# One more pair by Strassen's scheme, and sums that follow their banks, in a hybrid decoder layer

## The chip, the core and the metric

The kernel runs on one core of a Trainium2 chip. The metric is the device time of one launch in microseconds. Five engines work side by side, each through its own instructions in order: TensorE (PE in the profile; PEld is its load of the stationary operand), VectorE (DVE), ScalarE (ACT), GpSimd (POOL) and SyncE (SP, whose queue issues the DMAs). TensorE writes into eight banks of the accumulator memory (PSUM).

## What is computed

One layer of a decoder for 256 tokens of width 2048, all in f32:

```python
h = rmsnorm(x, norm_mix_g)
u = h @ w_in                       # 2048 x 12288, columns in fields of 1024 or 2048
ya = b_g * causal_dwconv3(c_g * xa, conv_w) * silu(za)
o  = hgrn2_chunked(silu(q), kk, iv, log_f)          # gated recurrence, 8 heads
yb = rmsnorm_per_head(o) * hg_norm_g * silu(og)
m  = sigmoid(ga) * (ya @ w_a_out) + sigmoid(gb) * (yb @ w_b_out)
x  = x + m @ w_o
gate = sigmoid(rmsnorm(x, ple_norm_g) @ w_ple_gate)
x  = x + gate * (p @ w_ple_proj)
return rmsnorm(x, final_norm_g)
```

The matrix products carry nearly all the work. `w_ple_gate` is called the gate in the title of the change and PG in the kernel; `ga` and `gb` are the two merge gates.

## The kernel before

**Products in three passes.** Both operands of a product are split into a high part (rounded to the format that TensorE takes, `F32R`) and a low part (the rest), and a product is the sum of high x high, high x low and low x high. ScalarE makes the high part of the weights (`whi`, L151), VectorE the low one (`wlo`, L152). The 256 tokens are two halves of 128 (t = 0, 1); a bank holds 128 tokens x 512 columns.

**Order of the work.** The columns of all weights are cut into groups of 512; the list `groups` (L169) has them in the order PP (w_ple_proj, whose results are kept in DRAM), the fields of w_in, then for each merge gate column j: ga, gb, A (w_a_out), B (w_b_out), then four groups O (w_o) and four groups PG (w_ple_gate). A group has 8 steps (A and B: 4); a step multiplies a chunk of 256 rows, two tiles of 128, so 2 tiles x 2 token halves x 3 passes = 12 matmuls of 512 columns. The weights come in units of 1 MB, two steps each, into three buffers (`raw`, L106). The split parts sit in a ring of four buffers, five around the pairs of gates (`more`, L206), and ten in PG, where a pool `late` of six joins the four.

**Looking ahead.** Ahead of a step's products, the loop at L1154 asks for all splits up to `ahead(pos)` steps further (L1093): three, four around the pairs, and in PG growing to eight, because the last PG group is multiplied token half by token half and needs all its eight steps split. After the products `ask_ahead` (L1104) asks for the loads of the next units, and `advance` (L1085) moves each open epilogue, a generator, on to its next `yield`. The framework's planner then sets the final order on each engine: it goes by what is ready in its own reckoning, and by program order among that.

**A pair.** For j = 1, 2, 3 the groups ga and gb are one pair GG of 24 steps (`PAIR`, L42). Four of its eight units are joint (`"S"`): one chunk of 256 rows by 1024 columns, that is two row tiles by two column groups, multiplied for both token halves by Strassen's scheme (in Winograd's form) with seven block products for eight. For it the weights are combined (`combine_weights`, L159: three VectorE instructions L163, L166, L167), and so is the left operand (`forms`, L720). A joint unit has four parts with 6, 3, 6 and 6 matmuls. The other four units are plain, each for one of the two column groups. All eight banks are used: four for the results (t, group) and four for the products 1, 5, 6, 7 that several results share. They are asked for at the pair's first step (L1194). `ep_pair` (L754) adds them up; it starts after the last joint unit's fourth part (L1199), and its first adds free the bank that group A needs right after the pair.

**O and PG.** `ep_o` (L816) adds a group of O to x, transposes it by way of DRAM (`turned`) and puts it into `x1T`, PG's left operand, scaled by the norm's gain (`put`, L249). `ep_pg` (L857) takes the sigmoid of a PG group, multiplies it with the kept projection (`load_projection`, L1055, two buffers), adds to x and sums squares; GpSimd multiplies by the final gain (L875). The last group is multiplied in the loop behind the main one (L1257), one bank at a time.

Of the kernel before, what the change touches and what calls it, by code (L numbers as in the profile page):

```python
# [9 lines left out]
F32 = mybir.dt.float32  # L10
F32R = mybir.dt.float32r
# [4 lines left out]
P = 128  # L16
# [25 lines left out]
PAIR = ("S", 0), (0, 2), ("S", 1), (1, 2), ("S", 4), (0, 6), ("S", 5), (1, 6)  # L42
PAIRED = [c for u, c in PAIR if u == "S"]

# [3 lines left out]
PAD_CONST, PAD_SMALL = 8, 64  # L48
# [3 lines left out]
def hybrid_kernel(ctx, tc, xT, x, pT, prm, gfin, masks, w_in, w_a, w_b, w_o, w_pg, w_pp, out):  # L52
# [77 lines left out]
    def split(pos, c0=0, c1=2 * CW):  # L130
# [9 lines left out]
        if more(pos) and pos % (4 + MORE) < MORE:  # L140
            pool, n = pools["tmp2"], MORE
# [29 lines left out]
    for n, (kind, j) in enumerate(IN_ORDER):  # L171
        if j == 0 or kind not in ("ga", "gb"):
            groups.append((kind, j, w_in, n, "hT"))
        elif kind == "ga":
            groups.append(("GG", j, w_in, n, "hT"))
# [14 lines left out]
    for gi, (kind, j, w, g, op) in enumerate(groups):  # L190
        if kind != "GG":
# [3 lines left out]
        for n, (u, c) in enumerate(PAIR):  # L195
# [7 lines left out]
    first_pair = min(pos for pos, s in enumerate(joint) if s)  # L203
    last_pair = max(pos for pos, s in enumerate(joint) if s)

    def more(pos):  # L206

        return first_pair - 12 <= pos <= last_pair + 8
# [511 lines left out]
    def forms():  # L720


        for n in range(0, len(PAIRED), 2):
            raw, f = t4(), t4()
            r = raw.rearrange("p (u k t) -> p u k t", u=2, k=2)
            for u in range(2):
                c = PAIRED[n + u]
                nc.sync.dma_start(out=r[:, u], in_=xT[:, 2 * c : 2 * c + 2, :])
            for u in range(2):
                yield  # L730
                for k in range(2):
                    h = r[:, u, k, :]
                    nc.scalar.activation(
                        out=h, in_=h, func=AF.Identity, scale=gain(PRM_GMIX, 2 * PAIRED[n + u] + k)
                    )
            yield
            a11, a12, a21, a22 = (r[:, :, k, t * P : (t + 1) * P] for t in range(2) for k in range(2))
            s1, s2, s3, s4 = (f[:, i * 2 * P : (i + 1) * 2 * P].rearrange("p (u t) -> p u t", u=2) for i in range(4))
            nc.vector.scalar_tensor_tensor(out=s1, in0=a21, scalar=-1.0, in1=a22, op0=ALU.mult, op1=ALU.subtract)
            nc.vector.scalar_tensor_tensor(out=s2, in0=s1, scalar=-1.0, in1=a11, op0=ALU.mult, op1=ALU.subtract)  # L740
            yield
            nc.vector.tensor_tensor(out=s3, in0=a11, in1=a21, op=ALU.subtract)
            nc.vector.tensor_tensor(out=s4, in0=a12, in1=s2, op=ALU.subtract)
            yield
            hi, lo = (pools["tmp2"].tile([P, 1024], F32R, tag="S" + x, bufs=2, name=nm("S" + x)) for x in "hl")
            nc.scalar.activation(out=hi, in_=f, func=AF.Copy)
            nc.vector.tensor_tensor(out=lo, in0=f, in1=hi.bitcast(F32), op=ALU.subtract)
            for u in range(2):
                for i in range(4):
                    s = slice((2 * i + u) * P, (2 * i + u + 1) * P)  # L750
                    state["S", PAIRED[n + u], i] = hi[:, s], lo[:, s]
            yield

    def ep_pair(j, e, m):  # L754

        ga, gb = t4("ga", 1), t4("gb", 1)
        state["ga", j], state["gb", j] = ga, gb
        a, b = slice(0, CW), slice(CW, 2 * CW)

        def add(out, x, y):  # L760
            nc.vector.tensor_tensor(out=out, in0=x, in1=y, op=ALU.add)

        nc.scalar.activation(out=gb[:, a], in_=m[1], func=AF.Copy)
        add(ga[:, a], gb[:, a], e[0, 0])
        add(gb[:, a], gb[:, a], m[6])
        yield
        add(gb[:, b], gb[:, a], m[7])
        add(ga[:, b], gb[:, b], e[1, 0])
        yield
        pair = gb.rearrange("p (t c) -> p t c", t=2)  # L770
        add(pair, pair, m[5].rearrange("p (o c) -> p o c", o=1).to_broadcast([P, 2, CW]))
        for t in range(NT):
            s = slice(t * CW, (t + 1) * CW)
            nc.scalar.activation(
                out=ga[:, s], in_=ga[:, s], func=AF.Sigmoid, scale=state["rstd1"][:, t : t + 1]
            )
        yield
        for t in range(NT):
            s = slice(t * CW, (t + 1) * CW)
            add(gb[:, s], gb[:, s], e[t, 1])  # L780
        yield
        for t in range(NT):
            s = slice(t * CW, (t + 1) * CW)
            nc.scalar.activation(
                out=gb[:, s], in_=gb[:, s], func=AF.Sigmoid, scale=state["rstd1"][:, t : t + 1]
            )
# [29 lines left out]
    def ep_o(j, psum):  # L816
        xs = state["x"]
        x1 = t4()
        for t in range(NT):
            d = xs[:, t, j * CW : (j + 1) * CW]  # L820
            nc.vector.tensor_tensor(out=d, in0=d, in1=psum[t], op=ALU.add)
# [12 lines left out]
        x1 = yield from turn  # L834
        for c in range(4):
# [21 lines left out]
    def ep_pg(j, psum):  # L857
        xs, pw, gt = state["x"], state["pw", j], t4()
# [493 lines left out]
```

## Time and profile before

| what | value |
|---|---|
| median of 3 runs | 817.11 us (816.95 to 817.17) |
| the profiled execution's own time | 816.79 us |
| its span, first to last instruction | 815.0 us |
| mean granted TensorE clock | 0.996 |
| PE, DVE, ACT, POOL busy | 804.8, 603.9, 455.8, 91.1 us |
| three gate pairs start at | 443.55, 506.26, 569.29 us, 40.80 us each |
| PG starts at, its last group at | 719.04, 784.32 us |
| last matmul ends at | 806.9 us |

Times within the profile count from the span's start. A line such as `L152 DVE TENSOR_TENSOR wlo<-raw,whi ... x302 | 379.8, 1273 | 168.2 <-ACT whi L151` is a group of instructions: kernel line, engine, operation, what it writes and reads, how many; then busy time in us and the mean of one in ns; then the engine's idle time ahead of them, with what ended it. In a table by stage each row is a stretch of the span: its length, each engine's busy time and instructions, the granted clock, the DMA share and GB/s. The chain of waits is followed back from the last instruction.

### The profile page before, as it was taken

The page shows a single profiled execution, that of the slowest core. Times are in us where ns is not written, and L with a number is a line of the kernel's source. Part 1 is how long each engine was busy: PE and PEld are TensorE (multiplying, and loading weights), DVE is VectorE, ACT ScalarE, POOL GpSimd, SP SyncE. Part 2 cuts the span into 40 slices and gives each one's busy share as a digit, 9 for nine tenths or more (in the row PEclk, how much of TensorE's full clock was granted, in tenths as well). Part 3 has the DMA queues.
Part 4 walks back from the last instruction along what each step waited for, and adds up shares of the span by engine and source line. Part 5 has one row for each costly group of instructions (what it writes and reads, how often), then busy time and mean ns, then how long its engine had stood idle before and what let it go on. Part 6 is the DMA issues. An engine that isn't in the chain of part 4 may idle for free.

```text
span 815.0 us, 10926 instructions
## 1 busy us (share of the span) xinstructions
PE 804.8 (99%) x4199; PEld 668.8 (82%) x4200; DVE 603.9 (74%) x711; ACT 455.8 (56%) x596; POOL 91.1 (11%) x75
## 2 busy tenths in 40 slices
PE   9999999999999999999999999999999999999996
PEld 7888888888888888888888888888888888888885
DVE  6746697967766498967768998998996656679734
ACT  7666465555565465465664565554564455567522
POOL 1000045400000055200001001000100000001210
PEclk9999999999999999999999999999999999999998
DMA  9969655647767555748764774774765788887702
GB/s 341 375 267 335 231 176 205 232 158 240 255 236 249 201 178 191 225 153 262 265 232 155 236 278 142 226 272 144 252 256 170 260 296 298 285 285 280 296 1 104
DMA packets 45556, 188.32 MB, mean 231 GB/s; under 512 B 5184, under 2 KB 14656, under 8 KB 29888
## 3 DMA queue, kind: packets, MB, share of 16 engines
q1 hardware_dynamic: 45360, 187.36, 66.1%
q8 instruction: 33, 0.54, 0.3%
q10 hardware_dynamic: 144, 0.26, 0.1%
q14 instruction: 19, 0.16, 0.1%
HBM read 173.97 MB, written 13.63 MB: 230 GB/s over the span
## 4 chain that ended last, share of the span: by engine, by line
PE 93%; DVE 3%; issue 1%; DMA 1%; ACT 1%; ACTq 0%; POOLq 0%; POOL 0%
PE g L1102 80%; PE g L1122 7%; PE s L1122 3%; DVE wlo L152 2%; ACT whi L151 1%; PE s L1102 1%; PE s L448 1%; DMA raw<-in_w_a 1%; DMA raw<-in_w_pp 1%; DVE raw L163 0%; DVE t L166 0%; PE s L581 0%; PE s L604 0%; PE s L605 0%; PE s L603 0%
## 5 line engine op out<-in xcount | busy, mean ns | idle before, releaser
L152 DVE TENSOR_TENSOR wlo<-raw,whi 128x1024 fp32r<-128x1024 f32 (+1 forms) x307 | 382.5, 1262 | 168.4 <-ACT whi L151 165.3
L151 ACT ACTIVATE whi<-raw 128x1024 fp32r<-128x1024 f32 (+1 forms) x307 | 317.1, 1049 | 254.1 <-PE g L1102 205.7
L1102 PE MATMUL g<-wlo,xh 128*128 128x512 f32 (+1 forms) x720 | 276.7, 384 | 0.0
L1102 PE MATMUL g<-whi,xl 128*128 128x512 f32 (+1 forms) x720 | 276.7, 384 | 0.0
L1102 PE MATMUL g<-whi,xh 128*128 128x512 f32 (+1 forms) x720 | 276.3, 385 | 0.0
L1102 PEld LDWEIGHTS g<-whi,xl 128*128 128x128 f32 x720 | 135.3, 188 | 27.0
L1102 PEld LDWEIGHTS g<-wlo,xh 128*128 128x128 f32 x720 | 135.3, 188 | 26.8
L1102 PEld LDWEIGHTS g<-whi,xh 128*128 128x128 f32 x720 | 135.3, 188 | 26.6
L1102 PE MATMUL g<-whi,mh 128*128 128x512 f32 x128 | 49.8, 389 | 0.0
L1102 PE MATMUL g<-wlo,mh 128*128 128x512 f32 x128 | 49.8, 389 | 0.0
L1102 PE MATMUL g<-whi,ml 128*128 128x512 f32 x128 | 49.6, 389 | 0.0
L1122 PE MATMUL g<-whi,xh 128*128 128x512 f32 x120 | 46.7, 389 | 0.0
L1122 PE MATMUL g<-wlo,xh 128*128 128x512 f32 x120 | 46.7, 389 | 0.0
L1122 PE MATMUL g<-whi,xl 128*128 128x512 f32 x120 | 46.7, 389 | 0.0
L151 ACT ACTIVATE whi<-t 128x512 fp32r<-128x512 f32 x12 | 7.6, 634 | 49.5 <-DVE t L166 49.5
L804 POOL TENSOR_TENSOR t<-ga,gb 128x512 f32<-128x512 f32 x6 | 10.6, 1786 | 193.6 <-issue 118.7
L1102 PE MATMUL g<-whi,yaTh 128*128 128x512 f32 (+1 forms) x74 | 28.0, 389 | 1.1 <-ACT whi L151 0.9
L1102 PEld LDWEIGHTS g<-whi,mh 128*128 128x128 f32 x128 | 24.0, 188 | 5.0
L1102 PEld LDWEIGHTS g<-whi,ml 128*128 128x128 f32 x128 | 24.0, 188 | 5.0
L1102 PEld LDWEIGHTS g<-wlo,mh 128*128 128x128 f32 x128 | 24.0, 188 | 4.9
L502 POOL TENSOR_TENSOR t<-b 128x512 f32<-128x512 f32 x10 | 20.3, 2034 | 68.5 <-DMA t<-turn 41.0
L1102 PE MATMUL g<-wlo,yaTh 128*128 128x512 f32 (+1 forms) x74 | 28.0, 384 | 0.0
(202 smaller groups left out, 860.6 us busy)
## 6 DMA issues: line engine op xcount, KB each, us to landing
raw<-in_w_in SPq DMA_DIRECT2D x73, 1024.0 KB, 4.8
raw<-in_w_in SPq DMA_DIRECT2D x34, 512.0 KB, 6.1
raw<-in_w_o SPq DMA_DIRECT2D x16, 1024.0 KB, 5.7
raw<-in_w_pg SPq DMA_DIRECT2D x16, 1024.0 KB, 5.3
turn<-t SPq DMA_DIRECT2D x72, 128.0 KB, 2.6
t<-turn SPq DMA_DIRECT2D x18, 512.0 KB, 5.2
raw<-in_w_a SPq DMA_DIRECT2D x8, 1024.0 KB, 5.2
raw<-in_w_b SPq DMA_DIRECT2D x8, 1024.0 KB, 6.4
```

Of the source, the lines that this page charges most:

```text
L151: a = nc.scalar.activation(out=hi[:, s], in_=src[:, s], func=AF.Copy)
L152: v = nc.vector.tensor_tensor(out=lo[:, s], in0=src[:, s], in1=hi[:, s].bitcast(F32), op=ALU.subtract)
L448: nc.tensor.matmul(heads(bk)[r, h, c if at is None else slice(at, at + 32)], key(h)[:, r], query(h)[:, c], start=True, stop=True, tile_pos ...
L502: nc.gpsimd.tensor_tensor(out=er, in0=br, in1=ref, op=ALU.subtract)
L804: (nc.vector if j == 3 else nc.gpsimd).tensor_tensor(out=spread(m, t), in0=blocks(ga[:, s]), in1=blocks(gb[:, s]), op=ALU.add)
L1102: nc.tensor.matmul(psum, a, b, start=first and n == 0, stop=last and n == 2)
L1122: nc.tensor.matmul(banks[name], x, y[:, s], start=k == total[name] and i == 0, stop=k == 1 and i == 2)
```

## The change

PG's groups 1 and 2 become a pair GP, with its own order of units, `LATE`: plain (group 1, chunks 4 and 5), S0, plain (1, chunks 6 and 7), S1, plain (2, chunks 4 and 5), S2, S3, plain (2, chunks 6 and 7). The joint chunks 0 to 3 lie in the columns of x that O's groups 0 and 1 make, so `ep_o` builds the combined forms of `x1T` there, by the shared `forms`, and writes `x1T` itself as one copy and one subtraction for four chunks. The sums are one generator `sums` for both kinds of pair: it is opened ahead of the first joint unit and goes on as soon as the banks it reads are complete (`left` counts their products down). A bank is asked for at its first product. For GP, `gated` (the old body of `ep_pg`) takes the summed columns instead of banks; projections 1 and 2 are loaded in S0 and S1, projection 3 after the first of the two sums. The look-ahead in PG grows by one each three steps instead of four, and so reaches eight at the 20th of its steps (before: the 25th); the extra buffer around the gates is asked for a little earlier. A pad of 64 words in the small pool goes.

```diff
-PAIR = ("S", 0), (0, 2), ("S", 1), (1, 2), ("S", 4), (0, 6), ("S", 5), (1, 6)
+GATES = ("S", 0), (0, 2), ("S", 1), (1, 2), ("S", 4), (0, 6), ("S", 5), (1, 6)
+LATE = (0, 4), ("S", 0), (0, 6), ("S", 1), (1, 4), ("S", 2), ("S", 3), (1, 6)
-PAD_CONST, PAD_SMALL = 8, 64
+PAD_CONST, PAD_SMALL = 8, 0
...
-        t2 = half[unit_of[pos]] = pools["tmp2"].tile([P, CW], F32, tag="t2", bufs=2, name=nm("t2"))
+        t2 = half[unit_of[pos]] = pools["tmp2" if pos in gates else "tmp3"].tile([P, CW], F32, tag="t2", bufs=2 if pos in gates else 1, name=nm("t2"))
...
-    groups += [("PG", j, w_pg, j, "x1T") for j in range(4)]
+    groups += [("PG", 0, w_pg, 0, "x1T"), ("GP", 1, w_pg, 1, "x1T", LATE), ("PG", 3, w_pg, 3, "x1T")]
...
+    def sums(e, left, tiles_of, then):
+        def until(*names):
+            while any(left[n] for n in names):
+                yield
+        yield from until(1, 6, (0, 0))
+        ga, gb = tiles_of()
+        nc.scalar.activation(out=gb[:, A], in_=e[1], func=AF.Copy)
+        add(ga[:, A], gb[:, A], e[0, 0])
+        add(gb[:, A], gb[:, A], e[6])
+        yield
+        yield from until(7, (1, 0))
+        add(gb[:, B], gb[:, A], e[7])
+        add(ga[:, B], gb[:, B], e[1, 0])
+        yield
+        yield from until(5)
+        both = gb.rearrange("p (t c) -> p t c", t=2)
+        add(both, both, e[5].rearrange("p (o c) -> p o c", o=1).to_broadcast([P, 2, CW]))
+        then(0, ga)
+        yield
+        yield from until((0, 1), (1, 1))
+        add(gb[:, A], gb[:, A], e[0, 1])
+        add(gb[:, B], gb[:, B], e[1, 1])
+        yield
+        then(1, gb)
...
     def ep_o(j, psum):
...
+        if j < 2:
+            for c in range(4):
+                h = x1[:, c * T : (c + 1) * T]
+                nc.scalar.activation(out=h, in_=h, func=AF.Identity, scale=gain(PRM_GPLE, j * 4 + c))
+            hi, lo = (x[:, j * 4 : j * 4 + 4, :].rearrange("p k t -> p (k t)") for x in state["x1T"])
+            nc.scalar.activation(out=hi, in_=x1, func=AF.Copy)
+            nc.vector.tensor_tensor(out=lo, in0=x1, in1=hi.bitcast(F32), op=ALU.subtract)
+            yield
+            r = x1.rearrange("p (u k t) -> p u k t", u=2, k=2)
+            yield from forms("x1T", pools["tmp3"], f"So{j}", r, (2 * j, 2 * j + 1))
+            return
...
+    def ep_gates_late(j, e, left):
+        def then(q, g):
+            gate = gated(j + q, g, [g[:, A], g[:, B]])
+            next(gate)
+            active.append(gate)
+            if q == 0:
+                load_projection(3)
+        yield from sums(e, left, lambda: (t4(), t4()), then)
...
-        return LEAD + min(max(pos - (last_group - 20), 0) // 4, 5) + MORE * (first_pair - 8 <= pos <= last_pair + 8 - MORE)
+        return LEAD + min(max(pos - late - 4, 0) // 3, 5) + MORE * (more(pos + LEAD) is not None and more(pos + LEAD + MORE) == more(pos + LEAD))
...
         def add(name, xh, xl, s):
+            if name not in banks:
+                banks[name] = bank("g" if type(name) is tuple else "s")
...
             if c == (0, 0):
-                left = dict(total)
-                banks = {n: bank("g" if type(n) is tuple else "s") for n in total}
-            pair_products(c)
+                total = products_of(program)
+                left, banks = dict(total), {}
+            if c == (min(n for n, (u, _) in enumerate(program) if u == "S"), 0):
+                active.append({"GG": ep_pair, "GP": ep_gates_late}[kind](j, banks, left))
+            pair_products(c, program, opname)
             ask_ahead()
             if not joint[pos] or c[1] % 2:
                 advance()
-            if c == (max(n for n, (u, _) in enumerate(PAIR) if u == "S"), 3):
-                m = {n: banks[n] for n in (1, 5, 6, 7)}
-                active.append(ep_pair(j, banks, m))
-                step(active[-1])
+            if kind == "GP" and c in ((1, 1), (3, 1)):
+                load_projection(1 + c[0] // 2)
             continue
```

More of the change, by code (lines that the diff above doesn't have):

```diff
@@ L202, in hybrid_kernel @@
     LEAD, MORE = 3, 1
-    first_pair = min(pos for pos, s in enumerate(joint) if s)
-    last_pair = max(pos for pos, s in enumerate(joint) if s)
+    of_kind = lambda *kinds: [pos for pos, (gi, c) in enumerate(steps) if groups[gi][0] in kinds]
+    gates, late = of_kind("GG"), of_kind("PG")[0]
+    gates = range(gates[0] - 12, gates[-1] + 9)
     def more(pos):
-        return first_pair - 12 <= pos <= last_pair + 8
+        return "tmp2" if pos in gates else None
     TOKENS, NORM = 10, 13
@@ L739, in forms @@
-            nc.vector.scalar_tensor_tensor(out=s1, in0=a21, scalar=-1.0, in1=a22, op0=ALU.mult, op1=ALU.subtract)
-            nc.vector.scalar_tensor_tensor(out=s2, in0=s1, scalar=-1.0, in1=a11, op0=ALU.mult, op1=ALU.subtract)
+            yield from forms("hT", pools["tmp2"], f"Sx{n}", r, chunks)
             yield
[L742 to L765, printed above, removed]
+    def add(out, x, y):
+        nc.vector.tensor_tensor(out=out, in0=x, in1=y, op=ALU.add)
@@ L788, in ep_a, with ep_pair, tiles_of @@
+    def ep_pair(j, e, left):
+        def tiles_of():
+            state["ga", j], state["gb", j] = t4("ga", 1), t4("gb", 1)
+            return state["ga", j], state["gb", j]
+        def then(q, g):
+            for t in range(NT):
+                s = slice(t * CW, (t + 1) * CW)
+                nc.scalar.activation(
+                    out=g[:, s], in_=g[:, s], func=AF.Sigmoid, scale=state["rstd1"][:, t : t + 1]
+                )
+        yield from sums(e, left, tiles_of, then)
     def ep_a(j, psum):
@@ L1148, in hybrid_kernel @@
         first_of.setdefault(u, q)
-    plain = [4 * sum(u == i for u, _ in PAIR) for i in range(2)]
-    total = {(t, g): plain[g] + len(PAIRED) * ((t, g) != (1, 1)) for g in range(2) for t in range(NT)}
-    total.update({n: len(PAIRED) for n in (1, 5, 6, 7)})
     psum = None
     for pos, (gi, c) in enumerate(steps[:last_group]):
-        kind, j, w, g, opname = groups[gi]
+        kind, j, w, g, opname, *program = groups[gi]
         nch = w.shape[2]
```

99 lines of the change are left out of this document (52 added, 47 removed).

## The prediction

> **What bounds the kernel now.** I read the page's busy shares first, then the chain in order of time, then tables by stage, and last VectorE's groups and timelines.
>
> ```profile
> span 815.0 us, 10926 instructions
> PE 804.8 (99%) x4199; PEld 668.8 (82%) x4200; DVE 603.9 (74%) x711; ACT 455.8 (56%) x596; POOL 91.1 (11%) x75
> ...
> L151 ACT ACTIVATE whi<-raw 128x1024 fp32r<-128x1024 f32 (+1 forms) x307 | 317.1, 1049 | 254.1 <-PE g L1102 205.7
> ```
>
> TensorE is busy for 99% of the span (L151, ScalarE's half of a split, serves below), and the chain shows at what pace:
>
> ```profile
> 16.62 119.68 PE g L1102 x528
> ...
> 484.51 21.92 PE g L1102 x96
> ...
> 521.14 1.23 DVE wlo L152
> ...
> 522.39 1.24 DVE raw L163
> ...
> 523.65 0.70 DVE t L166
> ...
> 530.83 1.23 DVE wlo L152
> ...
> 547.63 0.61 DVE ga L761
> 548.24 0.04 issue
> 548.28 21.17 PE g L1102 x92
> ```
>
> 528 products took 119.68 us, 0.2267 us each. In the stretch 521 to 548 the chain leaves TensorE and runs through VectorE: there, at the end of the second pair, TensorE waits for a sum (L761) that frees a bank. By stage (the four A groups first, then a whole gate pair, PG's groups 0 to 2, the last group, the tail):
>
> ```profile
> core 0: us, PE busy (x) PEld busy (x) DVE busy (x) ACT busy (x) POOL busy (x), PEclk, DMA share, GB/s
> 421.79:432.67 10.88, 10.88 (x49) 9.01 (x48) 7.61 (x10) 5.97 (x7) 0.00 (x0) 1.00 0.59 198
> 484.35:495.38 11.03, 11.03 (x50) 8.93 (x48) 8.14 (x10) 6.08 (x7) 0.00 (x0) 1.00 0.62 214
> 547.06:558.41 11.35, 11.19 (x50) 8.93 (x48) 8.45 (x10) 6.09 (x7) 0.00 (x0) 1.00 0.60 208
> 610.09:621.12 11.03, 11.03 (x50) 8.93 (x49) 6.76 (x8) 5.02 (x6) 0.00 (x0) 1.00 0.62 212
> ...
> 506.26:547.06 40.80, 40.80 (x182) 33.78 (x181) 38.23 (x38) 24.03 (x26) 3.53 (x2) 1.00 0.72 252
> ...
> 653.76:675.52 21.76, 21.76 (x98) 18.02 (x97) 13.70 (x16) 12.25 (x18) 0.00 (x0) 1.00 0.80 270
> ...
> 719.04:740.80 21.76, 21.76 (x98) 18.02 (x97) 16.39 (x20) 14.61 (x21) 1.61 (x1) 1.00 0.87 298
> 740.80:762.56 21.76, 21.76 (x98) 18.02 (x97) 17.86 (x16) 13.80 (x18) 3.83 (x2) 1.00 0.83 315
> 762.56:784.32 21.76, 21.76 (x98) 18.02 (x97) 11.89 (x11) 9.92 (x14) 4.31 (x2) 1.00 0.35 136
> 784.32:806.90 22.58, 22.55 (x145) 20.47 (x143) 8.31 (x26) 4.88 (x11) 3.64 (x4) 1.00 0.12 47
> 806.90:815.00 8.10, 0.00 (x0) 0.00 (x0) 2.56 (x7) 1.81 (x3) 0.54 (x1) 0.63 0.34 129
> ```
>
> The reader is to see that TensorE has no free time in any stage, that a gate pair keeps VectorE busy for 38.23 of 40.80 us and yet costs TensorE nothing inside, and that PG leaves VectorE room. So the time is the count of products times their pace, plus a few waits, plus a tail of 8.1 us.
>
> **The change part by part.**
>
> *Fewer products.* A joint unit has 7 block products in three passes, 21 matmuls, for 24. Four units save 12: 12 x 0.2267 = 2.72 us. All of it is on the path, since PG's stages are full.
>
> *Sums that follow the banks.* The A group after no pair takes 10.88 us; those after a pair take 11.03, 11.35 and 11.03, so the pairs' ends cost 0.15 + 0.47 + 0.15 = 0.77 us. Before, the sums start after the last joint unit's fourth part; now the first two adds follow its second part, and each later one comes one step sooner: 12 products, 2.7 us, in either case. That is over the longest wait, so all 0.77 goes. What is late next is the pair's own splits behind the sums; they are asked for four steps ahead, so they stand in front of them in VectorE's queue. Bounds: 0 if the sums keep their place, and 1.1 us by the waits view:
>
> ```profile
> PEld g L1102 <- DVE ga L761: 1.1, 3, 0.6
> ```
>
> *VectorE in the late pair.* A joint unit adds to the split of its parts (three of 1024, one of 512) the three combinations L163, L166, L167:
>
> ```profile
> L152 DVE TENSOR_TENSOR wlo<-raw,whi 128x1024 fp32r<-128x1024 f32 x6 | 7.0, 1220 | 0.3 <-ACT whi L151 0.3
> L163 DVE TENSOR_TENSOR raw<-raw 128x1024 f32<-128x1024 f32 x1 | 1.2, 1226 | 0.0
> L152 DVE TENSOR_TENSOR wlo<-t,whi 128x512 fp32r<-128x512 f32 x1 | 0.7, 694 | 0.1
> L166 DVE TENSOR_TENSOR t<-raw 128x512 f32<-128x512 f32 x1 | 0.7, 692 | 0.0
> L167 DVE TENSOR_TENSOR raw<-raw,t 128x512 f32<-128x512 f32 x1 | 0.7, 691 | 0.0
> ```
>
> By busy time a unit is 3 x 1.17 + 1.2 + 3 x 0.7 = 6.8 us. By the chain above it is 7.4: from one joint unit's first split (521.14) to the next one's (530.83) are 9.7 us, and a plain unit's two splits take 2.3 of them. TensorE takes only 21 x 0.2267 = 4.76 us for it, and 5.44 for a plain unit. The gates alternate the two; the late order has S2 and S3 back to back, which is the place to watch. I keep a ledger on the clock of the run before, from rows of its PG:
>
> ```profile
> 731.41 1.23 DVE L152 TENSOR_TENSOR wlo<-raw,whi 128x1024 fp32r<-128x1024 f32 x1 [3.31 <-ACT whi L151]
> ...
> 736.52 4.63 DVE L152 TENSOR_TENSOR wlo<-raw,whi 128x1024 fp32r<-128x1024 f32 x4
> 742.45 1.32 DVE L866 TENSOR_TENSOR t<-t,pw 128x512 f32<-128x512 f32 x2 [1.30 <-ACT t L863]
> 743.69 1.29 DVE L867 TENSOR_TENSOR xs<-xs,t 128x512 f32<-128x512 f32 x2
> ...
> 744.89 9.11 DVE L152 TENSOR_TENSOR wlo<-raw,whi 128x1024 fp32r<-128x1024 f32 x6
> ...
> 745.68 3.83 POOL L875 TENSOR_TENSOR xs<-xs,gfin_t 128x512 f32<-128x512 f32 x2 [17.03 <-ACT t L868]
> ```
>
> At 736.52 VectorE starts the splits of PG's steps 10 to 13, which become S0. From there it owes four joint units, two plain ones (4.6), group 0's gate (1.32 + 1.29 = 2.6) and what GpSimd's two products cost it: the six splits beside them took 9.11 for 7.0, 2.1 more. So S3's last split ends at 736.5 + 9.3 + 4s: 773.0 with s = 6.8, 775.4 with 7.4, and its third part is 1.2 earlier, at 771.8 or 774.2. TensorE wants that third part at 719.04 + 10 x 2.72 + three joint and two plain units (25.2) + 9 x 0.2267 = 773.4. VectorE is thus 1.6 us early or 0.8 late. I take no stall: the 0.6 us between the two values of s are waits for ScalarE, which ten part buffers (five in the gates) let other splits fill, and the gate pair, the nearest stage, carries 94% without a stall. Ends kept: 0 and +0.8.
>
> *The pair's end.* PG's last group needs the bank of (0, 0) at 719.04 + 21.76 + 40.80 = 781.6. The add that frees it is queued behind splits up to that group's fourth, and the raw buffer of the third and fourth is that of S3, free at 773.0. With its load (row below), a wait for ScalarE of 1.0 and two splits of 1.2 it is 773.0 + 5.3 + 1.0 + 2.4 = 781.7, then a copy and an add of 0.7 each: 783.1, a wait of 1.5. If the planner lets the add pass those splits, there is none. I take 0 (VectorE would else idle from 778 on), and keep +1.5.
>
> *Behind the pair.* A sum's add has this row:
>
> ```profile
> L761 DVE TENSOR_TENSOR gb<-gb,s 128x512 f32<-128x512 f32 x6 | 4.1, 683 | 0.1
> ```
>
> VectorE owes the last plain unit and the last group (10 splits, 11.7), the sums (six adds of 0.68 and one twice as wide, 1.2: 5.3), one more gate (2.6), two more collisions (2.1) and the last stage's own 8.31: 30.0 us from 773.0 to TensorE's new end, 806.9 - 2.7 = 804.2, that is 31.2 us. It fits by 1.2; with s = 7.4 the final output is 1.2 late. I take 0, and keep +1.2. The sums read one operand from a bank, and no row shows such an add beside GpSimd. By the Trainium skill (SBUF — State Buffer, Who interferes with whom) only a VectorE instruction with two inputs in SBUF contends with a GpSimd that reads SBUF; the slowed splits have two, so the trace agrees. By that rule the two new collisions could fall on sums and cost nothing, and this end would be 0 in place of +1.2; by the row it stays.
>
> *Covered work.* The forms of x1T are made in O: two copies and lo of 1024 for four small ones, and four sums, some 2.4 us more of VectorE for each of two groups, covered by the 8 us that O leaves free (13.70 of 21.76). Without that cover x1T comes late to PG, at 2.4 us a time. The loads are as many bytes; a joint one is cut in three:
>
> ```profile
> raw<-in_w_pg SPq DMA_DIRECT2D x16, 1024.0 KB, 5.3
> ```
>
> The gates' joint ones, so cut, take 6.1:
>
> ```profile
> raw<-in_w_in SPq DMA_DIRECT2D x34, 512.0 KB, 6.1
> ```
>
> S3's buffer comes free with S1's last split (736.5 + 2s + 7.0, the plain unit, gate and collisions: 757.1 or 758.3) and is wanted s before S3's end, at 766.2 or 768.0: some 9 us for 6.1. SP's three issues for one and the three moved projections stand ahead of loads that wait for buffers anyway. The pad taken from the small pool moves addresses by 256 bytes; L166 and L167 take 692 and 691 ns at different addresses, so 0.
>
> **Sum.** -2.72 - 0.77 = -3.49. The profiled run is 816.79 us (span 815.0 and 1.8 around); it becomes 813.30. The median of the runs lies 0.32 above it: 813.6.
>
> **The rivals.**
> *S2 and S3 stall, or the bank does* (+0.8 or +1.5, at most both): 814.4 to 815.9. For it speaks the chain through VectorE in the second gate pair; against it the full TensorE in that row.
> *The change gives nothing net*: VectorE binds from S2 to the end, +0.8 + 1.5 + 1.2 at once: 817.1. For: 30.0 of 31.2 us owed. Against: every term at its bad end.
> *Slower: the early sums get in the way.* At all four pairs' ends, if the planner puts the adds ahead of the last plain unit's splits, VectorE waits until TensorE is through S's fourth part, then does two adds (1.4) and a split (1.2) while TensorE, at the next unit, wants that split at once: 2.6 a pair, 10.4 in all, 817.1 - 3.5 + 10.4 = 824.0. It decides for slower from 5.1 in all, 1.3 a pair. Against: splits are asked for first.
> *The clock falls.* In the tail, where TensorE idles, the granted clock is 0.63 over 8.1 us. If VectorE came in with no lead at S2, TensorE would idle 2 x (7.4 - 4.76) = 5.3 us, and a like dip would cost 8.1 x 0.37 = 3.0: 813.6 + 8.3 = 821.9. Against: the first split of the pair is ready 8 us early (731.41 + 1.23 against 740.80). The Trainium skill (TensorE: Matmul & The Clock Gate, Part 1) states such a rule, half the clock after an idle window of about 3.4 us; the tail's 0.63 agrees, and no loaded stage shows it.
>
> **How the numbers follow.** Forecast 0.52; stall 0.20; nothing net 0.10; early sums 0.15; clock 0.03. A measurement here tells 0.2%, 1.6 us, from no change: faster is below 815.5, slower above 818.7. The stall rival lies three quarters on the faster side of 815.5: faster 0.52 + 0.15 = 0.67, same 0.05 + 0.10 = 0.15, slower 0.18. The range runs from 813.0 (1.1 for 0.77, and the runs' spread of 0.2) to 817.3 (817.1 and that spread); that leaves out the 0.18. The forecast's own range is 813.0 to 814.5.
>
> **What would show it.** 12 fewer matmuls in PG; all three later A groups at 10.88 us; the late pair at 40.80 with VectorE near 95%; the waits of TensorE's loads for L761's successor gone. The forecast is wrong if TensorE waits for a split of S2 or S3, for the add that frees the last group's bank, or if the tail behind the last product is longer than 8.1 us.

## The result

| | before | after |
|---|---|---|
| median, us | 817.24 | 815.21 |
| ratio, with its 95% interval | 1 | 0.9972 (0.9964 to 0.9980) |
| median of a second set of runs, us | 817.54 | 815.38 |
| its ratio | 1 | 0.9973 (0.9963 to 0.9984) |

The change makes the kernel faster by 0.28% by the ratio. The medians lie 2.0 us apart, in the second set 2.2, where 3.5 were forecast. The time is inside the stated range, but not at the forecast's own place (813.0 to 814.5). The page of after, whose first lines are the span and the busy shares:

```profile
span 815.5 us, 10972 instructions
## 1 busy us (share of the span) xinstructions
PE 803.9 (99%) x4187; PEld 668.2 (82%) x4188; DVE 630.9 (77%) x742; ACT 465.1 (57%) x609; POOL 90.6 (11%) x74
```

TensorE has 12 matmuls fewer, VectorE 31 instructions and 27.0 us more (603.9 before). The profiled execution (817.31 us) is a slow one of its kind: its first product of w_in comes 1.7 us later than in a second profile of the same kernel, most of it because TensorE started at half pace (last section). I therefore read it by stages, beside that second profile. Four instants carry the account (us from each span's start):

| | before | after | after, second profile |
|---|---|---|---|
| first product of w_in | 16.46 | 18.21 | 16.56 |
| first product of O | 632.00 | 632.96 | 631.38 |
| last product starts | 806.59 | 805.77 | 804.29 |
| end | 815.01 | 815.52 | 813.15 |
| from w_in to O | 615.54 | 614.75 (-0.79) | 614.82 (-0.72) |
| from O to the last product | 174.59 | 172.81 (-1.78) | 172.91 (-1.68) |
| from the last product to the end | 8.42 | 9.75 (+1.33) | 8.86 (+0.44) |

The table by stage of after, in the columns of the one before: the three later A groups with the second gate pair among them, O's group 1, PG's group 0, the late pair, the wait behind it, the last group, the tail.

```profile
core 0: us, PE busy (x) PEld busy (x) DVE busy (x) ACT busy (x) POOL busy (x), PEclk, DMA share, GB/s
486.08:496.96 10.88, 10.88 (x50) 9.01 (x48) 7.89 (x9) 5.72 (x7) 0.00 (x0) 1.00 0.70 245
507.84:548.64 40.80, 40.80 (x182) 33.78 (x180) 38.54 (x39) 24.36 (x27) 3.53 (x2) 1.00 0.71 244
548.64:559.52 10.88, 10.88 (x50) 9.01 (x48) 7.89 (x9) 5.72 (x7) 0.00 (x0) 1.00 0.69 246
611.20:622.08 10.88, 10.88 (x50) 9.01 (x48) 7.89 (x9) 5.72 (x7) 0.00 (x0) 1.00 0.68 245
654.72:676.48 21.76, 21.76 (x98) 18.02 (x96) 13.63 (x16) 13.73 (x20) 0.00 (x0) 1.00 0.79 266
720.00:741.76 21.76, 21.76 (x98) 18.02 (x96) 16.98 (x22) 14.22 (x21) 1.61 (x1) 1.00 0.89 312
741.76:782.56 40.80, 40.80 (x181) 33.60 (x179) 37.68 (x37) 23.85 (x31) 3.99 (x2) 1.00 0.58 209
782.56:783.43 0.87, 0.27 (x2) 0.11 (x1) 0.77 (x3) 0.87 (x2) 0.00 (x0) 1.00 0.81 339
783.43:806.00 22.57, 22.57 (x144) 20.47 (x144) 20.75 (x36) 9.61 (x19) 6.81 (x5) 1.00 0.08 30
806.00:815.50 9.50, 0.05 (x1) 0.00 (x0) 3.69 (x13) 2.43 (x5) 1.09 (x2) 0.78 0.58 221
```

The first column is the stretch, the second its length. The A groups take 10.88 us, all of them, and the late pair 40.80 with TensorE busy throughout: both gains are there. Two rows are worse than before. Behind the pair stands a stretch of 0.87 us in which TensorE does next to nothing. And in the last group VectorE is busy for 20.75 us of 22.57 where it was 8.31, and the tail is 1.4 us longer.

**The wait behind the pair.** From the timeline of after; a row is start, length, engine, line, operation, what it writes and reads, count, and in brackets the idle time ahead of it with what ended that:

```profile
774.34 0.33 SPq L118 DMA_DIRECT2D raw<-in_w_pg  x1
...
773.10 5.76 DVE L152 TENSOR_TENSOR wlo<-raw,whi 128x1024 fp32r<-128x1024 f32 x5
780.31 2.36 DVE L152 TENSOR_TENSOR wlo<-raw,whi 128x1024 fp32r<-128x1024 f32 x2 [1.45 <-ACT whi L151]
782.59 0.68 DVE L761 TENSOR_TENSOR t<-t,g 128x512 f32<-128x512 f32 x1
...
779.22 2.01 ACT L151 ACTIVATE whi<-raw 128x1024 fp32r<-128x1024 f32 x2 [2.74 <-DMA raw<-in_w_pg]
781.13 0.58 ACT L774 ACTIVATE t<-s 128x512 f32<-128x512 f32 x1
...
783.32 0.50 PE L1147 MATMUL g<-whi,xh 128*128 128x512 f32 x1 [0.60 <-DVE t L761]
```

The copy (L774) and the add (L761) that free the last group's bank read products that TensorE finished in S3's first two parts; twelve of S3's matmuls and a plain unit's 24 follow, so that was 8.2 us ahead of the pair's end. Yet they stand in the queues behind the splits of the last group's third and fourth steps, whose load was issued at 774.34 and landed about 779.2. Until then ScalarE idled 2.74 us and VectorE 1.45: both had time for the copy and the add, and their order kept them from using it.

**The tail.** VectorE and GpSimd of after, last group:

```profile
790.41 0.68 DVE L912 TENSOR_TENSOR xs<-xs,t 128x512 f32<-128x512 f32 x1
...
792.75 1.78 DVE L912 TENSOR_TENSOR xs<-xs,t 128x512 f32<-128x512 f32 x1
...
800.18 2.09 DVE L929 TENSOR_TENSOR t<-t,pw 128x256 f32<-128x256 f32 x2 [1.17 <-ACT t L928]
...
807.86 0.16 DVE L957 TENSOR_TENSOR xs<-tot,tot 128x1 f32<-128x1 f32 x1 [0.73 <-POOL tot L956]
807.93 0.42 DVE L929 TENSOR_TENSOR t<-t,pw 128x256 f32<-128x256 f32 x1
...
808.85 0.43 DVE L936 SCALAR_TENSOR_TENSOR t<-xs 128x257 f32<-128x257 f32 x1
...
791.93 2.05 POOL L920 TENSOR_TENSOR xs<-xs,gfin_t 128x512 f32<-128x512 f32 x1 [39.44 <-ACT t L913]
...
799.25 2.74 POOL L920 TENSOR_TENSOR xs<-xs,gfin_t 128x512 f32<-128x512 f32 x2 [2.59 <-ACT t L913]
```

The same addition takes 0.68 us alone and 1.78 beside GpSimd's product. VectorE runs late through the whole last group, so that the last square (L936 at 808.85) starts 3.08 us behind the last product's start at 805.77, where it was 1.74 before (808.33 and 806.59). The end of this delay is again one of order. The sigmoid of the final piece (L928) starts at 806.64, behind two scalings of the first token half on ScalarE, and takes 0.45 us; the product that needs it (L929) stands on VectorE behind the short instructions that close the sums so far (up to L957), and VectorE idles 0.73 us among them for a result of GpSimd (L956). Before, these were done at 804.5, 2.9 us ahead of the piece.

So, from the first product of w_in to the end: -0.79 and -2.72 as forecast, then some +0.9 at the pair's end and +1.33 in the tail, -1.2 in all. In the second profile the two losses are +1.0 and +0.44; with its -0.72 and -2.72 that is -2.0, and the medians say -2.0 and -2.2.

### The profile page after: what moved, and what is told of

Read it like the earlier page. It is cut to its first block, busy times and chain, and to the rows that moved or that the text cites. A ratio compares the mean times of both kernels' runs of the same rounds, so it can differ in the third digit from the quotient of the medians.

```text
span 815.5 us, 10972 instructions
## 1 busy us (share of the span) xinstructions
PE 803.9 (99%) x4187; PEld 668.2 (82%) x4188; DVE 630.9 (77%) x742; ACT 465.1 (57%) x609; POOL 90.6 (11%) x74
## 4 chain that ended last, share of the span: by engine, by line
PE 90%; DVE 5%; issue 1%; DMA 1%; ACT 1%; POOL 0%; ACTq 0%; POOLq 0%; DVEq 0%
PE g L1147 73%; PE g L1169 11%; PE s L1169 4%; DVE wlo L152 2%; PE s L1147 1%; PE s L450 1%; DMA raw<-in_w_pg 1%; DVE raw L163 1%; DVE t L911 1%; DMA raw<-in_w_pp 1%; DVE xs L912 0%; ACT whi L151 0%; DVE t L929 0%; DVE t L761 0%; DVE t L166 0%
## 5 line engine op out<-in xcount | busy, mean ns | idle before, releaser
L152 DVE TENSOR_TENSOR wlo<-raw,whi 128x1024 fp32r<-128x1024 f32 (+1 forms) x311 | 385.7, 1255 | 155.0 <-ACT whi L151 153.6
L1147 PE MATMUL g<-whi,xh 128*128 128x512 f32 (+1 forms) x656 | 251.8, 385 | 0.6 <-DVE t L761 0.6
L1147 PE MATMUL g<-wlo,xh 128*128 128x512 f32 (+1 forms) x656 | 251.9, 384 | 0.0
L1147 PE MATMUL g<-whi,xl 128*128 128x512 f32 (+1 forms) x656 | 251.7, 384 | 0.0
L1147 PEld LDWEIGHTS g<-whi,xh 128*128 128x128 f32 x656 | 123.3, 188 | 25.5 <-DVE t L761 1.0
L1147 PEld LDWEIGHTS g<-whi,xl 128*128 128x128 f32 x656 | 123.3, 188 | 24.5
L1147 PEld LDWEIGHTS g<-wlo,xh 128*128 128x128 f32 x656 | 123.3, 188 | 23.9
L1169 PE MATMUL g<-wlo,xh 128*128 128x512 f32 x160 | 62.2, 389 | 0.0
L1169 PE MATMUL g<-whi,xl 128*128 128x512 f32 x160 | 62.2, 389 | 0.0
L1169 PE MATMUL g<-whi,xh 128*128 128x512 f32 x160 | 62.1, 389 | 0.0
L1169 PEld LDWEIGHTS g<-whi,xl 128*128 128x128 f32 x160 | 30.0, 188 | 6.3
L1169 PEld LDWEIGHTS g<-whi,xh 128*128 128x128 f32 x160 | 30.0, 188 | 6.3
L1169 PEld LDWEIGHTS g<-wlo,xh 128*128 128x128 f32 x160 | 30.0, 188 | 6.2
L1147 PE MATMUL g<-whi,yaTl 128*128 128x512 f32 (+1 forms) x74 | 28.3, 390 | 0.0
```

The costliest lines, as they stand in the source:

```text
L152: v = nc.vector.tensor_tensor(out=lo[:, s], in0=src[:, s], in1=hi[:, s].bitcast(F32), op=ALU.subtract)
L1147: nc.tensor.matmul(psum, a, b, start=first and n == 0, stop=last and n == 2)
L1169: nc.tensor.matmul(banks[name], x, y[:, s], start=k == total[name] and i == 0, stop=k == 1 and i == 2)
```

## The experiments

My theory: TensorE's saving is all there, and two things hand part of it back, the order in VectorE's queue at the pair's end and the load on VectorE behind it, which GpSimd's products make heavier. The rivals: the early sums do harm; the loss is a matter of addresses or of the run; or it lies in the late pair's own splits. I first took the two halves of the change apart.

**The same kernel again.** No edit.

> The changed kernel as it is, for a second profile beside the others. Theory A (VectorE's queue): of the 3.49 us that were summed up, a wait of 0.8 to 1.0 us at the late pair's end and 1.2 to 1.5 us of VectorE backlog behind the last product are lost again, in this profile as in the first; the ratio to the kernel before is 0.997 to 0.9985. Theory B (the start): the first profile lost its 1.7 us in the slow first products alone; a profile with a normal start then ends 3 us or more ahead of the kernel before, tail and pair's end included.

815.38 us against 817.54, ratio 0.9973 (0.9963 to 0.9984). Its pair's end and its tail in the table by stage:

```profile
780.98:781.88 0.90, 0.16 (x2) 0.00 (x1) 0.84 (x2) 0.46 (x1) 0.00 (x0) 1.00 0.93 391
...
804.52:813.10 8.58, 0.05 (x1) 0.00 (x0) 2.83 (x10) 1.81 (x3) 1.09 (x2) 0.72 0.61 235
```

The wait at the pair's end is no accident of one execution; the tail varies, from 9.75 us to 8.86 in all, so that its loss here is 0.44 us and not the 1.2 to 1.5 expected.

**Only the sums.** PG stays four plain groups, with the look-ahead and the pad of before.

```diff
-PAD_CONST, PAD_SMALL = 8, 0
+PAD_CONST, PAD_SMALL = 8, 64
...
-    groups += [("PG", 0, w_pg, 0, "x1T"), ("GP", 1, w_pg, 1, "x1T", LATE), ("PG", 3, w_pg, 3, "x1T")]
+    groups += [("PG", j, w_pg, j, "x1T") for j in range(4)]
...
-        if j < 2:
+        if j < 0:
...
-        return LEAD + min(max(pos - late - 4, 0) // 3, 5) + MORE * (more(pos + LEAD) is not None and more(pos + LEAD + MORE) == more(pos + LEAD))
+        return LEAD + min(max(pos - (last_group - 20), 0) // 4, 5) + MORE * (more(pos + LEAD) is not None and more(pos + LEAD + MORE) == more(pos + LEAD))
...
+            if j == 2:
+                load_projection(3)
```

> Only the sums that follow their banks; PG stays four plain groups with the old look-ahead and pad. Theory A: the three A groups behind the pairs take 10.88 us each, so the span falls by 0.77 us (ratio 0.999), and PG and the tail are as before. Rival (the early sums get in the way): waits for splits appear at the gate pairs' ends, and the time is that of the kernel before or more.

816.38 against 817.54, ratio 0.9983 (0.9975 to 0.9992); the span is 0.8 us under that of before. The A group behind the second pair (11.35 before), from the table by stage:

```profile
546.88:557.76 10.88, 10.88 (x49) 9.01 (x48) 7.89 (x9) 5.72 (x7) 0.00 (x0) 1.00 0.72 251
```

The early sums bring their 0.77 us and do no harm; that rival falls.

**Only the late pair.** The sums of the gates start after the last joint unit, as before.

```diff
-            if c == (min(n for n, (u, _) in enumerate(program) if u == "S"), 0):
-                active.append({"GG": ep_pair, "GP": ep_gates_late}[kind](j, banks, left))
+            if kind == "GP" and c == (min(n for n, (u, _) in enumerate(program) if u == "S"), 0):
+                active.append(ep_gates_late(j, banks, left))
...
+            if kind == "GG" and c == (max(n for n, (u, _) in enumerate(program) if u == "S"), 3):
+                active.append(ep_pair(j, banks, left))
+                step(active[-1])
```

> The late pair as changed, but at the three gate pairs the sums start after the last joint unit's fourth part, as in the kernel before. Theory A: A groups of 11.03, 11.35 and 11.03 us again, so 0.77 us more than the changed kernel, ratio to the kernel before 0.998 to 0.999; the late pair's end and the tail as in the changed kernel. Rival: the lost part of the forecast lay in the gate pairs, then this one is as fast as the changed kernel.

816.00 against 817.54, ratio 0.9982 (0.9973 to 0.9991). Waits of TensorE's loads, from the view of waits (engine, line, what it waited for: us in total, times, longest):

```profile
PEld g L1147 <- DVE ga L761: 1.3, 3, 0.7
PEld g L1147 <- DVE t L761: 1.2, 1, 1.2
```

The waits for the gates' sums (`ga`) are back, and that for the late pair's (`t`) is there too. The late pair brings 1.5 us where its 12 products are worth 2.72: the loss belongs to it alone. By the medians the two halves bring 1.2 and 1.5, the whole 2.2.

**A shorter look-ahead.** Six steps at most in place of eight, so that fewer of the last group's splits are asked for ahead of the sums.

```diff
-        return LEAD + min(max(pos - late - 4, 0) // 3, 5) + MORE * (more(pos + LEAD) is not None and more(pos + LEAD + MORE) == more(pos + LEAD))
+        return LEAD + min(max(pos - late - 4, 0) // 3, 3) + MORE * (more(pos + LEAD) is not None and more(pos + LEAD + MORE) == more(pos + LEAD))
```

> The look-ahead in PG grows to six steps, not eight, so that the first two sums stand ahead of the splits of the last group's third and fourth steps on VectorE and ScalarE. Theory A: TensorE's wait at the late pair's end (0.88 us) goes, and VectorE uses the 1.4 us in which it waited for that load, so the tail shortens by 1 us or more: 1.5 to 2.2 us less than the changed kernel, ratio to the kernel before 0.9955. Rival (the last group starves): its splits come too late, TensorE waits in the last group, no gain.

814.82 against 817.54, ratio 0.9966 (0.9952 to 0.9979). By the medians that is 0.56 us under the kernel after, though the intervals overlap, and less than the 1.5 to 2.2 expected. Its timeline:

```profile
777.41 0.68 DVE L761 TENSOR_TENSOR t<-t,g 128x512 f32<-128x512 f32 x1
...
779.00 2.36 DVE L152 TENSOR_TENSOR wlo<-raw,whi 128x1024 fp32r<-128x1024 f32 x2
...
788.55 0.50 PE L1147 MATMUL g<-wlo,xh 128*128 128x512 f32 x1 [0.16 <-DVE wlo L152]
```

The add now runs at 777.41, in the time in which VectorE idled, ahead of the two splits, and the wait behind the pair is gone. So that wait came from the add's place behind these two splits. Some of it comes back: the last group waits for a split at 788 (0.43 us beyond a product's pace) and for another at 791 (0.23), and from O to the last product it takes 172.58 us, only 0.2 to 0.3 less than after. The tail is 2.17 us (last product's start to last square), as in the second profile of after (2.19).

**Look-ahead six, then eight.** The same with 8 again from the pair's last units on (`5 if pos > late + 27 else 3`).

> Look-ahead of six steps until the first sums are queued, eight from there on. The wait for the bank at the pair's end stays away (as with six throughout), and the 0.3 us that TensorE waited for a split in the last group with six throughout should go: 0.3 to 0.5 us less than six throughout, ratio to the kernel before 0.996. If the splits delay the later sums and with them the tail, no gain over six throughout.

815.16 against 817.25, ratio 0.9979 (0.9970 to 0.9988), where some 0.996 was expected. There is no wait at the pair's end; instead there is one of 1.32 us beyond a product's pace at 790.2, for a split, and a tail of 2.25. The wait only moved: the order decides where TensorE waits, and with none of the three settings of the look-ahead (eight, six, six then eight) does it go without a wait.

**GpSimd's products left out.** The final gain of the groups 1 and 2 isn't multiplied (L920).

```diff
-            nc.gpsimd.tensor_tensor(out=d, in0=d, in1=state["gfin"][:, j * CW : (j + 1) * CW], op=ALU.mult)
+            if j == 0:
+                nc.gpsimd.tensor_tensor(out=d, in0=d, in1=state["gfin"][:, j * CW : (j + 1) * CW], op=ALU.mult)
```

> The changed kernel without GpSimd's products with the final gain for the columns of the late pair (groups 1 and 2), so these columns of the output lack that factor; group 0 keeps its. It takes the collisions of GpSimd with VectorE out of the last 20 us and leaves the rest. If the collisions carry the tail (theory A1): VectorE's L912, L911 and L929 take 0.4 to 0.7 us again, and the last square starts 1.7 us after the last product's start, as in the kernel before (2.2 to 3.1 in the changed one): 0.4 to 1.3 us less than the changed kernel; the wait at the pair's end stays 0.9. If the tail is VectorE's sheer count of instructions (A2): no more than 0.2 us less.

814.41 against 817.25, ratio 0.9969 (0.9957 to 0.9982). The wait at the pair's end is unchanged (1.2 us in the view of waits, 1.0 and 1.2 in the two profiles of after), and the tail is back to 1.74. VectorE's products and additions of the gates there (busy us in all, mean ns), first in after, then in this kernel, whose lines lie one further on:

```profile
L912 DVE TENSOR_TENSOR xs<-xs,t 128x512 f32<-128x512 f32 x4 | 3.7, 955 | 0.0
L911 DVE TENSOR_TENSOR t<-t,pw 128x512 f32<-128x512 f32 x4 | 3.2, 829 | 0.2 <-ACT t L908 0.2
L929 DVE TENSOR_TENSOR t<-t,pw 128x256 f32<-128x256 f32 x4 | 2.9, 750 | 1.2 <-ACT t L928 1.2
```

```profile
L911 DVE TENSOR_TENSOR t<-t,pw 128x512 f32<-128x512 f32 x4 | 2.7, 689 | 0.2 <-ACT t L908 0.2
L912 DVE TENSOR_TENSOR xs<-xs,t 128x512 f32<-128x512 f32 x4 | 2.7, 685 | 0.0
L930 DVE TENSOR_TENSOR t<-t,pw 128x256 f32<-128x256 f32 x4 | 1.6, 426 | 2.7 <-ACT t L929 2.7
```

9.8 us against 7.0: GpSimd costs VectorE 2.8 us there. In the second profile of after the three rows sum to 9.1, that is 2.1, and its tail was shorter by 0.9. Without that cost the tail to the last square is that of before, and the wait at the pair's end stands: the two parts of the loss are separate, and this is the second.

**Both at once.** The look-ahead of six, and the final gain of group 2 (`if j == 2: return` ahead of L920) moved into VectorE's last scaling, which then takes two groups' columns. The pieces of the output are cut and ordered anew for it, and ScalarE's queue issues one of their DMAs.

> Look-ahead of six steps, and the final gain of group 2's columns moves from GpSimd into the last scaling (VectorE's, which already does so for group 3; ScalarE scales groups 0 and 1). It takes two of the four late collisions away. If the collisions hold the tail: the last square starts 1.7 us after the last product's start (2.2 with six steps alone), 0.2 to 0.5 us less than six steps alone, the rest of it given back by the longer last scaling (2 x 0.75 for 2 x 0.35 + 0.75 on VectorE). If VectorE's count of instructions holds it, the same as six steps alone or slower.

814.45 against 817.26, ratio 0.9967 (0.9955 to 0.9978). The last square starts 1.75 us behind the last product, but from that product to the end it still takes 8.8 us, as with six steps alone: the longer last scaling gives back what was gained. A split is waited for at 788.2 for 0.5 us beyond the pace. By the intervals it is no better than either edit alone. The collisions went the other way here: L911 and L912 kept their 0.69 us, while GpSimd's two remaining products took 3.93 us each (1.54 on average in after). So which engine loses when the two meet isn't the same in every kernel.

**The pair first.** The pair is PG's groups 0 and 1, with the plain group 2 behind it, so that no plain group ahead of the pair lets VectorE gather a lead, and the bank freed by the sums is wanted by group 2.

```diff
-LATE = (0, 4), ("S", 0), (0, 6), ("S", 1), (1, 4), ("S", 2), ("S", 3), (1, 6)
+LATE = (0, 4), ("S", 0), (1, 4), ("S", 1), (0, 6), ("S", 2), ("S", 3), (1, 6)
...
-    groups += [("PG", 0, w_pg, 0, "x1T"), ("GP", 1, w_pg, 1, "x1T", LATE), ("PG", 3, w_pg, 3, "x1T")]
+    groups += [("GP", 0, w_pg, 0, "x1T", LATE), ("PG", 2, w_pg, 2, "x1T"), ("PG", 3, w_pg, 3, "x1T")]
...
```

The edit also moves the loads of the projections, and in the pair's first unit the epilogues go on ahead of the requests for loads.

> The late pair takes PG's groups 0 and 1 in place of 1 and 2 and a plain group follows it, so its sums, gates and GpSimd products have 22 us more before the end. Theory A (VectorE's backlog at the end and the bank behind the sums are what ate the gain): no wait at the pair's end over 0.1 us, the tail as in the kernel before (1.7 us from the last product's start to the last square), 3.3 to 3.6 us less than the kernel before, ratio 0.9957. Rival: without PG's group 0 ahead of it VectorE lacks the lead, TensorE waits for splits of S0 or S1, and it is no faster than the changed kernel.

820.54 against 817.25, ratio 1.0046 (1.0033 to 1.0059): slower, as its rival had it. TensorE waits five times between 739 and 767. The longest, at the pair's end, by the chain of waits (start, us, what):

```profile
757.21 4.86 DMA raw<-in_w_pg
...
762.17 1.07 ACT whi L151
...
764.40 1.22 DVE wlo L152
765.62 0.61 DVE t L761
...
766.27 3.90 PE g L1146 x9
```

It is the mechanism of after again, three times as long: a late load, two splits, then the add. Its own tail is 1.74. So a pair without a plain group ahead of it costs some 5 us against after (its lead in splits, the time to finish x1T's forms behind O and the adapted order weren't told apart). The tail's loss is gone where the pair doesn't lie next to the last group.

**Another order of units.** Joint and plain units alternate, as in the gates.

```diff
-LATE = (0, 4), ("S", 0), (0, 6), ("S", 1), (1, 4), ("S", 2), ("S", 3), (1, 6)
+LATE = ("S", 0), (0, 4), ("S", 1), (0, 6), ("S", 2), (1, 4), ("S", 3), (1, 6)
```

> The late pair in the alternating order S0, plain, S1, plain, S2, plain, S3, plain. If the adjacent S2 and S3 cost nothing (my forecast's ledger), the pair is as long as before, 40.8 us with the wait at its end near 1 us, and the time is that of the changed kernel within 0.3 us; if the adjacency cost VectorE its margin, the wait at the end and the tail shrink by up to 1 us.

816.62 against 817.25, ratio 0.9991 (0.9983 to 1.0000), the runs between 815.20 and 817.95; the profile is of one of 817.83. TensorE waits twice at 752 to 755 in S0, 1.3 us beyond the pace, behind VectorE's instructions that ran beside GpSimd's products for group 0, which fall in the pair's first steps:

```profile
744.28 3.46 DVE L152 TENSOR_TENSOR wlo<-raw,whi 128x1024 fp32r<-128x1024 f32 x2
747.77 2.20 DVE L163 TENSOR_TENSOR raw<-raw 128x1024 f32<-128x1024 f32 x1
```

Two splits take 3.46 us here for 2.36, and L163 takes 2.20 for 1.23. The tail is 4.37 us. The order of after, with S2 and S3 back to back and a plain unit in front, is the better one. Whether S2 and S3 side by side cost anything isn't told by this run, since it also takes away the plain unit ahead of S0.

**Half the joint units.** Two of them, S0 and S1; chunks 2 and 3 become plain, and only O's group 0 makes combined forms.

```diff
-LATE = (0, 4), ("S", 0), (0, 6), ("S", 1), (1, 4), ("S", 2), ("S", 3), (1, 6)
+LATE = (0, 4), ("S", 0), (0, 6), ("S", 1), (0, 2), (1, 2), (1, 4), (1, 6)
...
-        if j < 2:
+        if j < 1:
```

> The late pair with two joint units in place of four: plain (1, 4), S0, plain (1, 6), S1, then four plain units. 6 products less than the kernel before in place of 12: 1.36 us. Theory A (VectorE's surplus of a joint unit is paid at the pair's end and in the tail): with half of it, and four plain units behind S1, no wait of TensorE at the pair's end and the tail of the kernel before (1.7 us from the last product's start to the last square), so all of 1.36 + 0.77 = 2.1 us is gained and the time is that of the changed kernel within 0.4 us, ratio 0.9974. Rival (the wait and the tail come with any late pair): 1 to 2 us slower than the changed kernel.

814.43 against 817.26, ratio 0.9963 (0.9951 to 0.9976), the runs between 814.34 and 814.67. Its last group and tail in the table by stage, and the last piece from the timeline:

```profile
782.21:804.70 22.49, 22.49 (x145) 20.46 (x143) 13.29 (x31) 5.44 (x13) 5.09 (x5) 1.00 0.13 48
804.70:812.64 7.94, 0.05 (x1) 0.00 (x0) 2.56 (x7) 1.81 (x3) 0.54 (x1) 0.65 0.34 132
```

```profile
805.29 0.43 DVE L929 TENSOR_TENSOR t<-t,pw 128x256 f32<-128x256 f32 x1 [2.87 <-ACT t L928]
```

From O to the last product it takes 173.23 us, 1.36 under before: six products, to the hundredth. There is no wait at the pair's end, and VectorE, with 13.29 us in the last group for 20.75, idles 2.87 us ahead of its last piece. Six products are saved and kept; the other six of after are saved and given back. It is faster than before, and by its median 0.8 to 0.95 us faster than after (815.21 and 815.38), where at most 0.4 was expected; but those weren't run in one set and their intervals overlap, and the two profiles lie 0.5 us apart (812.6 against 813.1).

**The pad.** The kernel before, without it (`PAD_SMALL = 0`).

> The kernel before without the pad of 64 words in the small pool, nothing else. Forecast's value for the pad: 0, so within 0.1% of the kernel before. If the pad's addresses matter, the sums alone and the changed kernel owe part of their gain or loss to it: more than 0.15% either way.

817.07 against 817.26, ratio 0.9999 (0.9989 to 1.0008): nothing, as costed.

## Why the prediction was right, and where not

*Fewer products, -2.72: right.* 12 matmuls less, and from O to the last product 172.81 us, which is 174.59 - 2.72 and the wait of 0.9.

*Sums that follow the banks, -0.77: right.* All three A groups at 10.88; -0.8 in the span when done alone.

*VectorE in the late pair, 0: right.* No wait within it; the pair is at 40.80 with VectorE at 92%, not 95%. The ledger had S3's last split ending at 773.0 or 775.4 on the clock of before. Its raw buffer is loaded anew from 774.34 in after, whose PG starts 0.96 later: 773.4, so of the two values of a unit the 6.8 us taken was the nearer.

*The pair's end, 0 with +1.5 kept: here the forecast's sum failed.* The prediction had the add at 783.1 if it stood behind the last group's third and fourth splits, and took 0 because VectorE would else idle from 778 on and the planner would let the add pass. VectorE did idle, from 778.86 to 780.31, and the add did not pass. It ended at 783.27, 782.3 on the clock of before, against 781.6 wanted. The path of the kept end was right in its steps (load 4.9 for 5.3, ScalarE 1.1, two splits 2.4, the add 0.7), but for the copy: it was counted with 0.7 and ran beside the splits. What was wrong in the forecast was the belief that idle time is filled. The wait is 0.87 to 0.90 by the tables. In cap6, where the add stands ahead of the two splits, it is gone, though 0.66 us come back as waits for splits in the last group.

*Behind the pair, 0 with +1.2 kept: mis-sized.* Measured +1.33 in one profile and +0.44 in the other. The 30.0 us owed of 31.2 left too little: VectorE lost 1.45 us in the wait for the load, and GpSimd's collisions cost 2.8 or 2.1 us for the 2.1 reckoned. The count by amount of work also passed over dependences: the last pieces can't begin before their products, so a lead of 1.2 us in the sum is no lead at the end, and the 0.73 us that VectorE waits for GpSimd ahead of the final piece stood in no term. no_gain shows that without the collisions this loss is gone. The Trainium skill (SBUF — State Buffer, Who interferes with whom) has a VectorE instruction, outside the modes in which it uses both its port pairs, contend with GpSimd's reads only if both its inputs are in SBUF. The slowed ones (L911, L912, L929; L152 and L163 in alternate) all have two such inputs, so the trace agrees. That the collisions fall on the sums and cost nothing, which the prediction drew as one possibility, didn't come.

*Covered work, 0: right.* O's group 1 stays at 21.76 with the new forms, PG starts without a wait (at 720.00, four groups of 21.76 behind 632.96), and the pad is worth nothing.

The time belongs to the stall rival (814.4 to 815.9, chance 0.20), at the bank, with a part of the tail. The range holds it only because it was drawn out to the rivals; the forecast's own sum gave 813.6, 1.6 us less than measured. The rival by which the change gives nothing net didn't come: its first term stayed at 0, and its second at 0.9 of 1.5. The early sums did no harm. The clock didn't fall behind a wait in after; in pair_first it did, see below.

## What to carry to other kernels

A stage can run with its second engine at 92% and wait for nothing, as the late pair did; what that engine then owes must still fit into the stages behind it. Here two joint units kept all they saved, and the other two gave it back behind the pair. Idle time ahead of a late load doesn't fill itself where the order on a queue is set beforehand: ask which short instruction that frees a bank stands behind a split whose data is still on its way, and whether the last piece of the output stands behind a wait that isn't its own. The runs also suggest placing a pair that loads the second engine between two stages that let it rest: after lacks the one behind it, pair_first the one ahead. No run here has both.

## What the hardware showed

**The clock after a wait.** In pair_first the wait of 2.6 us is followed by products at half pace. Its table by stage (the wait and the time after it) and TensorE's timeline:

```profile
763.64:766.27 2.63, 0.16 (x1) 0.00 (x0) 2.58 (x3) 1.55 (x3) 0.00 (x0) 1.00 0.98 411
766.27:769.97 3.70, 3.70 (x9) 2.89 (x10) 3.65 (x5) 3.08 (x5) 0.00 (x0) 0.55 0.85 286
```

```profile
767.41 0.63 PE L1146 MATMUL g<-whi,xh 128*128 128x512 f32 x1
767.84 0.63 PE L1146 MATMUL g<-wlo,xh 128*128 128x512 f32 x1
```

Nine products take 3.70 us, most of them 0.43 us apart for 0.227, at a granted clock of 0.55; then the pace is full again. Some 1.7 us are lost. The Trainium skill (TensorE: Matmul & The Clock Gate, Part 1) gives half the clock after an idle window of about 3.4 us and full clock after as long a busy one; the time at half pace, some 3.4 us from 766.6 to 769.97, agrees with that, while the wait ahead of them was shorter, 2.6 us, with four shorter waits in the 27 us before. That execution took 822.26 us and the median 820.54, so most executions of this kernel may not have had it; none of those was profiled.

**The start.** The first profile of after and the second, from the first product on:

```profile
5.46:9.05 3.59, 3.59 (x15) 3.39 (x16) 3.21 (x8) 2.75 (x5) 0.00 (x0) 1.00 1.03 386
```

```profile
5.02:8.60 3.58, 3.58 (x20) 3.31 (x20) 3.17 (x8) 2.29 (x5) 0.00 (x0) 1.00 1.02 390
```

15 products against 20 in the same time, though the granted clock is recorded as 1.00 in both. From the first product to the first of w_in it takes 12.75 us against 11.54, and the first product itself starts 0.44 later: so an execution's start alone can differ by 1.7 us, as much as half of what this change could bring.
